# The low halves of streamed weight blocks: an accumulating DMA onto the negated high half in place of a subtraction on VectorE

## Chip, cores and metric

The kernel runs on one core of a Trainium2 chip. The metric is device time in microseconds (us) for one launch; lower is better. Engines are called by their names or by the letters of the profile: PE is TensorE's matmul queue, PEld its weight loads, DVE VectorE, ACT ScalarE, POOL GpSimd, SP SyncE.

## What is computed

A backbone of two layers (DEPTH = 2, D_MODEL = 1024, D_FF = 2816) for two groups of tokens that share all weights: a prompt of 128 tokens and a grid of 512 tokens. The kernel takes all 640 tokens through a layer together. In float32, cut to what matters:

```
h = rms_norm(x, norm1_g) * (1 + scale1) + shift1
z = h @ w_in            # conv streams, q, k, v, scan input, three gates
merged = (sigmoid(g_conv) * (y_conv @ w_proj_conv)
          + sigmoid(g_attn) * (y_attn @ w_proj_attn)
          + sigmoid(g_ssm) * (y_ssm @ w_proj_ssm))
x = x + gate1 * (merged @ w_out)
h = rms_norm(x, norm2_g) * (1 + scale2) + shift2
x = x + gate2 * ((silu(h @ w_ffn_gate) * (h @ w_ffn_up)) @ w_ffn_down)
```

The shifts, scales and gates are products of a condition vector with `w_ada` (1024 x 6144 in each layer).

## The kernel before

**Products of halves.** TensorE multiplies in the format float32r, which keeps fewer bits than float32. So every operand x is split as x = hi + lo, both of which float32r can hold, and a product is made of three: hi x hi, hi x lo, lo x hi. `gemm` (lines 732 to 740) does this for a tile of 128 output channels: for each of 8 input blocks k it issues hi of the weights with hi of the activations (two matmuls of 320 tokens), hi with lo (two) and lo with hi (two), so a tile has 48 matmuls, and the low half of the weights is first used by the fifth.

**The weight stream.** All weights come from HBM in 370 blocks of up to 128 x 1024 words (512 KB), in the order of use, which `order` lists (lines 284 to 360). `w_load` (line 365) takes one of three raw tiles (`wr`) and issues the load on SyncE's queue. `converter` (line 376) makes the two halves of a block in one of three tiles `wh` of 2 x 1024 words: a cast on ScalarE writes the high half, a subtraction on VectorE the low half. Then it calls `w_load` again: the next load must wait until its raw tile has been read. 308 blocks are converted in this way. 62 blocks of `w_ada` ("ada" blocks) are not: TensorE reads them raw, in eight matmuls with the condition vector (`ada_prod`), and the raw tile is free after that. They stand between the other blocks: one after each tile of the attention projection ("pa", `w_proj_attn`) and of the output projection ("o", `w_out`) in both layers, in layer 0 also between gate ("fg") and up ("fu") tiles of the feed-forward and in the convolution streams.

**What sets the order.** The program is written out by a planner. Main products are a generator (`layer`), side work (conversion, scan, attention) are further ones, and `pump` emits a piece of side work where the class `Clock` estimates that it can start. The estimates only set the order in which instructions stand in each engine's queue; each queue runs in that order. The converter may run up to two blocks ahead of the tile in use. In `Clock`, a DMA on GpSimd's queue counts as 1 us of that queue and 2 us more until its data is there. Every instruction is issued by a helper, so all of them have line 130 in the profile, and groups are told apart by the names of the tiles: `wr` raw block, `wh` halves, `bps` a tile in PSUM, `c` any tile of activations.

The conversion as it stands before:

```
            act.copy(hl[:, 0, :n], t[:, :n])
            yield hl, "dve"
            sub(hl[:, 1, :n], t[:, :n], f32(hl[:, 0, :n]))
            wtile[i] = [hl[:, r, :n].rearrange("p (k m) -> p k m", k=nr) for r in range(2)]
            w_load()
```

Of the kernel before, what the change touches and what calls it, by code (L numbers as in the profile page):

```python
# [11 lines left out]
OP = mybir.AluOpType  # L12
# [11 lines left out]
T = 8  # L24
# [33 lines left out]
class Clock:  # L58
    """estimated times (ns) of the instructions emitted so far; they only decide the order in which
    independent pieces of work are emitted"""  # L60
# [8 lines left out]
    def ring(self, tag, name, n):  # L69
        """a new PSUM tile takes the slot that is free first"""  # L70
        slots = self.rings.setdefault(tag, [None] * n)
        i = min(range(n), key=lambda j: self.free(slots[j]))
        self.avail[name] = self.free(slots[i])
        slots[i] = name
# [6 lines left out]
    def slot(self, tag):  # L81
        """when a tile can be had; side work ("b") leaves some PSUM tiles to the main products ("m")"""
        slots = sorted(self.free(x) for x in self.rings.get("b" if tag == "m" else tag, [None]))
        return slots[min(self.spare, len(slots) - 1) if tag == "b" else 0]

    def ready(self, needs):
        """when an instruction can start: needs are what it reads, its engine, and the tag of a PSUM tile it takes"""
# [23 lines left out]
class Engine:  # L111
    """forwards instructions to an engine and notes them in the clock"""
# [55 lines left out]
def trunk_kernel(ctx: ExitStack, tc: tile.TileContext, a):  # L168
# [86 lines left out]
    def split(x):  # L255
        """x = hi + lo exactly, both representable as float32r"""
# [5 lines left out]
    def split4(x):  # L262
        """x / 4 in the same way, from and to a tile of tokens"""
# [38 lines left out]
    def ada_gap(n):  # L302
        """blocks of the modulation products for times at which TensorE would wait"""
# [3 lines left out]
    def ada_n(key):  # L307
        """blocks of the modulation products after a tile"""
# [67 lines left out]
    def converter():  # L376
        for i, (key, src, nr, ncol) in enumerate(order):
# [10 lines left out]
            yield hl, "dve"  # L388
            sub(hl[:, 1, :n], t[:, :n], f32(hl[:, 0, :n]))
# [15 lines left out]
    class Side:  # L405
        """work beside the main products: a generator that yields, before each piece, what the first instruction
        of the piece needs (see Clock.ready), or a condition to wait for"""
# [23 lines left out]
    def pump(need=(), until=None):  # L431
        """emits the side work that can start before the main products"""
# [52 lines left out]
    # conditions between zeros: a window puts them on the rows of a slot  # L485
# [21 lines left out]
    def ada_flush(l=None, *vs):  # L507
        """the collected half vectors: rows to channels, bias, derived scales"""
# [30 lines left out]
    def ada_mm(k, w, c, start, stop):  # L539
        """a product of the conditions, on the rows of the slot in the column group of k"""  # L540
# [4 lines left out]
    def ada_step():  # L545
        """one block of the modulation products, of the weight stream"""
# [20 lines left out]
    def ada_pre(n):  # L567
        """loads blocks for the gaps"""
# [10 lines left out]
    def ada_fill(n):  # L579
        """blocks while TensorE would wait"""  # L580
# [6 lines left out]
    def ada_load():  # L587
        """next block of shift and scale of the first norm"""
# [11 lines left out]
    def ada_start():  # L600
        """shift and scale of the first norm, with plain float32 products"""
# [26 lines left out]
    def rstd(s, fill=(0,)):  # L628
        """reciprocal root mean square of each token, tokens on partitions"""
# [14 lines left out]
    def norm_rows(s, fill=(0, 0, 0), after=None):  # L644
        """reciprocal root mean squares on all partitions"""
# [14 lines left out]
    def norm(s, xs, sc, sh, fill=(0, 0, 0)):  # L660
        """h = x * rstd * sc + sh with the (sc, sh) of each group, split"""
# [36 lines left out]
    def place_x(xt, xs, sqs):  # L698
        """the residual stream, channels on partitions, and its squares"""
# [32 lines left out]
    def gemm(ps, w, c0, acts, first=True, last=True):  # L732
        """channel-major: ps[:, h, :HN] += w[:, :, c0:c0+128]^T @ acts, three products of the halves"""
# [17 lines left out]
    def gated(ps, x, gt, k):  # L751
        """x += gate * ps"""
# [14 lines left out]
    def pair_gemm(key1, key2, acts, evac1, evac2):  # L767
        """two tiles side by side, for activations that are still being made"""
# [20 lines left out]
    def blend(merged, m, th, ps):  # L789
        """merged[m] += (1 + th) * ps"""  # L790
# [6 lines left out]
    def branch(l, gk, pk, hs, ys, merged, spill=False):  # L797
        """merged += gate * projection; the first sum waits in DRAM for the second"""
# [63 lines left out]
    def hv(t):  # L862
        """[head of the pair, token tile, component]"""
        return t.rearrange("p (h i d) -> p h i d", h=2, i=NT)

    def token_major(key, hs, out):
        """raw projections of all tokens to 4 heads: two tiles of a head pair each"""
# [21 lines left out]
    def qk_norm(raw, which):  # L889
        """RMS over each head, gain, rotation of the sample tokens, in place"""  # L890
# [49 lines left out]
    def attn_prep(l, A, raws, preps, done):  # L940
        """per kv head, on partitions (hi, lo component): queries, keys; and values, (hi, lo) along the free axis"""
# [101 lines left out]
    def attn_scores(preps, scores, exps, done):  # L1043
        """exponentials, in the order in which they are used: per kv head those of the sample tokens, by head and
        query tile, then those of the prompt tokens"""
        for b in range(4):
# [18 lines left out]
            # prompt tokens, all four heads  # L1065
# [14 lines left out]
    def attn_turn(probs, turned, done):  # L1080
        """transposed probabilities: of pairs of query tiles, and of the prompt tokens of four heads"""
# [19 lines left out]
    def attn_split(turned, pts, done):  # L1101
        """both halves of the transposed probabilities"""
# [13 lines left out]
    def attn_out(preps, pts, done, ya):  # L1116
        """weighted sums of the values"""
# [44 lines left out]
    S = {}  # L1162

    def exp_acc(o, x, t, r, ki):
        """accurate exp of small tiles"""
# [35 lines left out]
    def ssm_layer(l):  # L1201
        """per-layer S5 parameters on partitions (direction, state)"""
# [42 lines left out]
        # coefficient (a - 1) / lambda  # L1245
# [27 lines left out]
        # unit phase and modulus of a^T  # L1273
# [28 lines left out]
        # powers a^0..a^8  # L1302
# [613 lines left out]
```

## Time and profile before

| | us |
|---|---|
| two timed runs | 2647.67 and 2642.18 |
| median | 2644.93 |
| span of the profiled execution, first to last instruction | 2643.2 |
| TensorE matmul busy | 2554.0 |
| VectorE busy | 1580.0 |
| ScalarE busy | 1016.2 |

The profile is of one execution. Its span is the time that rows are summed against; the two timed runs lie 1.0 us below and 4.5 us above it. A row of a group gives the engine, the operation, output<-input tiles, sizes and count, then the busy time, the mean duration of one, and the idle time of the engine just before these instructions with what ended it. A row of a timeline gives start and duration in us, and how many instructions of one kind follow each other. Matmuls overlap in their pipeline, so the mean duration of one is longer than the step from one to the next.

### The profile page before, as it was taken

The page shows a single profiled execution, that of the slowest core. Times are in us where ns is not written, and L with a number is a line of the kernel's source. Part 1 is how long each engine was busy: PE and PEld are TensorE (multiplying, and loading weights), DVE is VectorE, ACT ScalarE, POOL GpSimd, SP SyncE. Part 2 cuts the span into 40 slices and gives each one's busy share as a digit, 9 for nine tenths or more (in the row PEclk, how much of TensorE's full clock was granted, in tenths as well). Part 3 has the DMA queues.
Part 4 walks back from the last instruction along what each step waited for, and adds up shares of the span by engine and source line. Part 5 has one row for each costly group of instructions (what it writes and reads, how often), then busy time and mean ns, then how long its engine had stood idle before and what let it go on. Part 6 is the DMA issues. An engine that isn't in the chain of part 4 may idle for free. (4 is left out here: it accounts for less than half of the span.)

```text
span 2643.2 us, 44920 instructions
## 1 busy us (share of the span) xinstructions
PE 2554.0 (97%) x18683; PEld 2460.0 (93%) x18683; DVE 1580.0 (60%) x2982; ACT 1016.2 (38%) x1835; POOL 0.2 (0%) x4
## 2 busy tenths in 40 slices
PE   6999999999899999999989999999998999999998
PEld 4899999999888999999989999989998989999998
DVE  5888887788744433233677897578776453333333
ACT  4334336566622421122253333466664242212222
POOL 0000000000000000000000000000000000000000
PEclk8999999999999999999989999999999999999999
DMA  9433321121057233333334233212211633223222
GB/s 266 133 110 110 110 76 54 60 69 41 9 168 215 75 110 88 88 112 105 89 119 113 66 112 102 74 51 69 59 41 56 206 113 88 62 75 88 72 63 73
DMA packets 404411, 250.53 MB, mean 95 GB/s; under 512 B 57768, under 2 KB 392432, under 8 KB 404208
## 3 DMA queue, kind: packets, MB, share of 16 engines
q1 hardware_dynamic: 404208, 247.66, 31.9%
q8 instruction: 147, 2.41, 0.4%
q14 instruction: 56, 0.46, 0.1%
HBM read 227.49 MB, written 20.12 MB: 94 GB/s over the span
## 5 line engine op out<-in xcount | busy, mean ns | idle before, releaser
L130 PE MATMUL bps<-c,wh 128*128 128x320 f32 x12672 | 1952.1, 312 | 37.9 <-ACT c L130 18.4
L130 PEld LDWEIGHTS bps<-c,wh 128*128 128x128 f32 x12672 | 1876.4, 189 | 75.9 <-issue 25.1
L130 DVE TENSOR_TENSOR wh<-wr,wh 128x1024 fp32r<-128x1024 f32 (+2 forms) x308 | 353.8, 1153 | 223.6 <-ACT wh L130 213.8
L130 DVE TENSOR_TENSOR c<-c,c 128x512 f32<-128x512 f32 (+10 forms) x722 | 407.5, 590 | 71.6 <-ACT c L130 62.1
L130 ACT CAST wh<-wr 128x1024 fp32r<-128x1024 f32 (+2 forms) x308 | 303.7, 990 | 318.1 <-PE bps L130 177.9
L130 DVE SCALAR_TENSOR_TENSOR c<-c,bps 128x640 f32<-128x640 f32 (+1 forms) x108 | 83.2, 771 | 245.9 <-ACT c L130 169.6
L130 ACT CAST c<-c 128x640 fp32r<-128x640 f32 (+3 forms) x172 | 102.3, 621 | 327.0 <-DVE c L130 322.4
L130 DVE TENSOR_TENSOR c<-c,bps 128x640 f32<-128x640 f32 (+1 forms) x108 | 82.8, 769 | 205.9 <-PE bps L130 202.6
L130 PE MATMUL bps<-wh,c 128*128 128x256 f32 x1440 | 181.0, 284 | 2.0 <-ACT c L130 1.8
L130 ACT ACTIVATE c<-bps 128x640 f32<-128x640 f32 (+1 forms) x108 | 71.7, 664 | 285.3 <-PE bps L130 274.7
L130 PE MATMUL bps<-ident,c 128*128 128x128 f32 (+1 forms) x1115 | 159.1, 280 | 19.6 <-DVE c L130 7.4
L130 PEld LDWEIGHTS bps<-wh,c 128*128 128x128 f32 x1440 | 175.4, 191 | 2.7 <-ACT c L130 2.2
L130 PE MATMUL bps<-c,c 128*128 128x320 f32 (+2 forms) x960 | 159.5, 297 | 8.3 <-ACT c L130 4.5
L130 PEld LDWEIGHTS bps<-ident,c 128*128 128x128 f32 (+1 forms) x1115 | 132.6, 145 | 30.2 <-issue 8.9
L130 PEld LDWEIGHTS bps<-c,c 128*128 128x128 f32 x960 | 134.3, 191 | 13.4 <-ACT c L130 9.6
L130 ACT COPY c<-bps 64x256 f32<-64x256 f32 (+7 forms) x210 | 85.5, 445 | 155.8 <-PE bps L130 154.3
L130 ACT ACTIVATE c<-c 128x640 f32<-128x640 f32 (+4 forms) x93 | 65.3, 716 | 206.7 <-DVE c L130 206.5
L130 ACT ACTIVATE c<-bps,mx 128x640 f32<-128x640 f32 (+1 forms) x160 | 113.3, 713 | 36.1 <-DVE mx L130 35.6
L130 DVE TENSOR_REDUCE mx<-bps 128x1 f32<-128x640 f32 (+1 forms) x136 | 109.6, 809 | 26.4 <-PE bps L130 26.1
L130 DVE TENSOR_TENSOR pt<-bps,pt 128x640 fp32r<-128x640 f32 (+1 forms) x136 | 109.1, 810 | 15.3 <-ACT pt L130 14.5
L130 ACT CAST pt<-bps 128x640 fp32r<-128x640 f32 (+1 forms) x136 | 92.3, 687 | 26.6 <-PE bps L130 25.7
L130 PE MATMUL bps<-pt,c 128*128 128x256 f32 (+1 forms) x656 | 96.0, 292 | 2.9 <-DVE pt L130 2.1
(98 smaller groups left out, 1072.7 us busy)
## 6 DMA issues: line engine op xcount, KB each, us to landing
wr<-in_w_in_dram SPq DMA_DIRECT2D x104, 512.0 KB
wr<-in_w_ada_dram SPq DMA_DIRECT2D x62, 512.0 KB
wr<-in_w_ffn_gate_dram SPq DMA_DIRECT2D x44, 512.0 KB
wr<-in_w_ffn_up_dram SPq DMA_DIRECT2D x44, 512.0 KB
c<-in_w_ada_dram SPq DMA_DIRECT2D x68, 256.0 KB
wr<-in_w_ffn_down_dram SPq DMA_DIRECT2D x32, 384.0 KB
wr<-in_w_ffn_down_dram SPq DMA_DIRECT2D x32, 320.0 KB
wr<-in_w_proj_attn_dram SPq DMA_DIRECT2D x16, 512.0 KB
```

The lines of the kernel that those rows point to most:

```text
L130: res = f(*args, **kw)
```

## The change

The subtraction on VectorE goes. ScalarE now writes two tiles for each block: the cast as before, and the same block with the factor -1 into the place of the low half, which leaves the negated high half there. A DMA on GpSimd's queue then adds the raw block to it in place, so that block minus high half is left. The converter no longer stops between the two steps, so both copies stand together in ScalarE's queue. The raw tile is now read by ScalarE twice and by the DMA, and `w_load` waits for the DMA. The rest of the diff takes out docstrings and comments, which change no instruction.

```
@@ converter @@
             act.copy(hl[:, 0, :n], t[:, :n])
-            yield hl, "dve"
-            sub(hl[:, 1, :n], t[:, :n], f32(hl[:, 0, :n]))
+            act.activation(hl[:, 1, :n], t[:, :n], AF.Copy, scale=-1.0)
+            pool.dma_start(f32(hl[:, 1, :n]), t[:, :n], accum_op=OP.add)
             wtile[i] = [hl[:, r, :n].rearrange("p (k m) -> p k m", k=nr) for r in range(2)]
             w_load()
```

SyncE's queue in the attention projection of layer 0, before. A load waits for whatever read the raw tile last: DVE is the subtraction, PE the eight matmuls of an ada block; a DMAHW name is an earlier load by SyncE.

```order
L130 DMA wr<-in_w_ada_dram 128x4x256 [waits DMAHW6_49,PE_49]
L130 DMA wr<-in_w_proj_attn_dram 128x8x128 [waits DMAHW7_49,PE_49]
L130 DMA wr<-in_w_ada_dram 128x4x256 [waits DMAHW0_49,DVE_49]
L130 DMA wr<-in_w_proj_attn_dram 128x8x128 [waits DMAHW2_49,DVE_49]
L130 DMA wr<-in_w_ada_dram 128x4x256 [waits DMAHW1_49,PE_49]
L130 DMA wr<-in_w_proj_attn_dram 128x8x128 [waits DMAHW4_49,DVE_49]
L130 DMA wr<-in_w_ada_dram 128x4x256 [waits DMAHW3_49,PE_49]
L130 DMA wr<-in_w_proj_attn_dram 128x8x128 [waits DMAHW6_49,DVE_49]
```

The same place now; a DMASW name is an accumulating DMA of GpSimd's queue, Activation is ScalarE.

```order
L130 DMA wr<-in_w_ada_dram 128x4x256 [waits DMAHW6_49,PE_49]
L130 DMA wr<-in_w_proj_attn_dram 128x8x128 [waits DMAHW7_49,PE_49]
L130 DMA wr<-in_w_ada_dram 128x4x256 [waits DMAHW0_49,DMASW7_49,Activation_49]
L130 DMA wr<-in_w_proj_attn_dram 128x8x128 [waits DMAHW1_49,PE_49]
L130 DMA wr<-in_w_ada_dram 128x4x256 [waits DMAHW2_49,DMASW0_49,Activation_49]
L130 DMA wr<-in_w_proj_attn_dram 128x8x128 [waits DMAHW3_49,PE_49]
L130 DMA wr<-in_w_ada_dram 128x4x256 [waits DMAHW4_49,DMASW1_49,Activation_49]
L130 DMA wr<-in_w_proj_attn_dram 128x8x128 [waits DMAHW5_49,PE_49]
```

The two kinds of load have changed places: a projection block now goes into the tile that an ada block's matmuls free, an ada block into the tile that a conversion frees.

ScalarE's queue among the gate and up tiles of layer 0, before. `c<-bps` is the tanh of a gate tile, `c<-c` the cast of a hidden tile.

```order
L130 CAST wh<-wr 128x1024 [waits DMAHW7_49,Activation_49]
L130 ACTIVATE c_9729<-bps 128x640 [waits PE_49]
L130 CAST wh<-wr 128x1024 [waits DMAHW0_49,Activation_49]
L130 CAST c_9847<-c_9729 128x640 [waits DVE_49]
L130 CAST wh<-wr 128x1024 [waits DMAHW2_49,Activation_49]
```

And now:

```order
L130 CAST wh<-wr 128x1024 [waits DMAHW7_49,DMASW0_49,Activation_49]
L130 ACTIVATE wh<-wr 128x1024
L130 ACTIVATE c_9812<-bps 128x640 [waits PE_49]
L130 CAST wh<-wr 128x1024 [waits DMAHW0_49,DMASW1_49,Activation_49]
L130 ACTIVATE wh<-wr 128x1024
L130 CAST c_9932<-c_9812 128x640 [waits DVE_49]
L130 CAST wh<-wr 128x1024 [waits DMAHW2_49,DMASW2_49,Activation_49]
L130 ACTIVATE wh<-wr 128x1024
```

The order of casts and tile work is the same; the negated copy stands right behind each cast, and the cast of an up block still follows the cast of a hidden tile.

## Rows read from the trace of the kernel before

**Rows 1.** The page, part 1: busy us, share of the span, instructions.

```profile
PE 2554.0 (97%) x18683; PEld 2460.0 (93%) x18683; DVE 1580.0 (60%) x2982; ACT 1016.2 (38%) x1835; POOL 0.2 (0%) x4
```

**Rows 2.** Groups by form: shapes and count | busy us, mean ns | idle before.

```profile
L130 PE MATMUL bps<-c,wh 128*128 128x320 f32 x12672 | 1952.1, 312 | 37.9 <-ACT c L130 18.4 <-DVE c L130 9.5 <-DVE wh L130 7.2
...
L130 DVE TENSOR_TENSOR wh<-wr,wh 128x1024 fp32r<-128x1024 f32 x244 | 297.5, 1222 | 141.0 <-ACT wh L130 131.3
L130 ACT CAST wh<-wr 128x1024 fp32r<-128x1024 f32 x244 | 254.5, 1046 | 196.0 <-DMA wr<-in_w_proj_attn_dram 78.8 <-PE bps L130 77.0 <-DMA wr<-in_w_out_dram 32.5
...
L130 ACT CAST c<-c 128x640 fp32r<-128x640 f32 x116 | 81.8, 727 | 327.0 <-DVE c L130 322.4 <-issue 3.6
...
L130 ACT ACTIVATE c<-c 128x640 f32<-128x640 f32 x56 | 41.3, 742 | 169.3 <-DVE c L130 169.2
```

**Rows 3.** Waits: engine, waited for: us in total, times, longest us.

```profile
PE bps L130 <- ACT c L130: 30.1, 27, 5.9
...
PE bps L130 <- DVE c L130: 25.2, 29, 3.2
```

**Rows 4.** Waits of SyncE's DMA queue, the longest.

```profile
SPq L130 <- DVE wh L130: 1353.7, 254, 27.8
```

**Rows 5.** Timeline of PE, attention projection of layer 0.

```profile
744.45 0.64 PE L130 MATMUL bps<-wr,csT 128*32 128x256 f32 x8
745.02 7.30 PE L130 MATMUL bps<-c,wh 128*128 128x320 f32 x48
752.25 0.64 PE L130 MATMUL bps<-wr,csT 128*32 128x256 f32 x8
```

**Rows 6.** Timeline of SyncE's queue there: the issue of loads.

```profile
741.62 0.37 SPq L130 DMA_DIRECT2D wr<-in_w_proj_attn_dram  x1
745.15 0.37 SPq L130 DMA_DIRECT2D wr<-in_w_ada_dram  x1
747.58 0.37 SPq L130 DMA_DIRECT2D wr<-in_w_proj_attn_dram  x1
```

**Rows 7.** Timeline of ACT there: in brackets idle time before, and what ended it.

```profile
745.24 1.05 ACT L130 CAST wh<-wr 128x1024 fp32r<-128x1024 f32 x1 [4.91 <-DMA wr<-in_w_proj_attn_dram]
752.58 1.05 ACT L130 CAST wh<-wr 128x1024 fp32r<-128x1024 f32 x1 [6.29 <-DMA wr<-in_w_proj_attn_dram]
```

**Rows 8.** The chain that ended last, scan of layer 1: start us, us, what.

```profile
1465.78 1.78 DMA yd<-c
...
1468.01 2.88 DMA c<-yd
```

**Rows 9.** Stretches: us, busy us (count) by engine, granted clock, DMA share, GB/s.

```profile
1000.00:1100.00 100.00, 100.00 (x690) 98.79 (x689) 29.93 (x46) 19.05 (x24) 0.00 (x0) 1.00 0.31 89
784.00:840.00 56.00, 54.54 (x392) 50.38 (x392) 26.19 (x41) 12.19 (x14) 0.00 (x0) 1.00 0.81 254
713.00:719.00 6.00, 3.80 (x17) 3.07 (x16) 3.59 (x8) 4.14 (x8) 0.00 (x0) 0.78 0.00 0
```

**Rows 10.** Timeline of ACT, gate and up tiles of layer 0.

```profile
905.44 0.73 ACT L130 CAST c<-c 128x640 fp32r<-128x640 f32 x1 [7.02 <-DVE c L130]
906.07 1.05 ACT L130 CAST wh<-wr 128x1024 fp32r<-128x1024 f32 x1
```

**Rows 11.** Timeline of PE there.

```profile
911.51 0.64 PE L130 MATMUL bps<-wr,csT 128*32 128x256 f32 x8
912.08 14.34 PE L130 MATMUL bps<-c,wh 128*128 128x320 f32 x96
```

**Rows 12.** Timeline of DVE, attention projection of layer 0.

```profile
746.32 1.23 DVE L130 TENSOR_TENSOR wh<-wr,wh 128x1024 fp32r<-128x1024 f32 x1
```

## Prediction

> **What bounds the kernel now.** I read the page's busy times first, then the groups by form, the waits, SyncE's own waits, and last the timelines of the two places where a weight block is late.
>
> The busy times say that TensorE is the bound: 2554.0 of 2643.2 us, so all its idle time together is 89.2 us, while VectorE has 1580.0 us, ScalarE 1016.2 us and GpSimd nothing [rows 1]. That is the first thing to see: VectorE is not the bound, and whatever is taken off it can give back at most what TensorE waits for today. The groups give the price list: the subtraction takes 1222 ns for a block of 1024 words, the cast 1046 ns; the 12672 matmuls on weight halves have only 37.9 us of idle time ahead of them, 7.2 us of it until the subtraction [rows 2]. In the waits TensorE waited 30.1 us for ScalarE's tiles and 25.2 us for VectorE's [rows 3]. These 62.5 us are all that a faster VectorE could touch.
>
> SyncE's row is the second thing to see: its load queue stood 1353.7 us, 254 times, until a subtraction had freed a raw block [rows 4]. That costs nothing while the block comes back in time. How near it is to being late shows in the attention projection of layer 0. A tile's 48 matmuls and the 8 of an "ada" block make a period of 752.25 - 744.45 = 7.80 us [rows 5]. The load of a projection block is issued at 741.62 and at 747.58 us [rows 6], and the casts that wait for those loads start at 745.24 and 752.58 us [rows 7]: 3.62 and 5.00 us of landing, 4.3 in the mean. So each such block has load, cast and subtraction, about 4.3 + 2.3 us, in a chain of 6.6 us that must fit into 7.8 us. This is where a longer conversion goes onto the path.
>
> **What the change removes, adds and moves.** For each of the 308 converted blocks it removes the subtraction: 244 of 1024 words at 1.222 us [rows 2] and 64 of 640 or 768 words, which in proportion are 54 us: some 352 us in all from VectorE. Nearly all of it lies beside TensorE's work. What goes for certain is the 7.2 us of waits for a subtraction. Of the 55.3 us of waits for VectorE's and ScalarE's tiles I give back 10 us: VectorE comes sooner, but ScalarE, which releases the larger part, gets more to do.
>
> It adds to ScalarE a negated copy. The nearest rows are a cast of 640 words, 727 ns, and an activation of 640 words, 742 ns [rows 2]; so I take 1.02 x 1046 = 1.07 us for 1024 words, about 308 us in all. ScalarE has room for that in the mean (1016 + 308 of 2643 us), and in the dense stages it waits for TensorE; the price is that the low half starts 1.07 us later.
>
> It adds a DMA from GpSimd's queue, which reads the raw block and the negated half and writes the sum. GpSimd issues nothing today [rows 1], so nothing else is queued behind it there; but everything that waits for the low half or for the raw block now waits for this DMA to land. Its time from the end of the copy to landing, call it X, is the unknown of this case. Bound below: the shortest DMA on the chain of waits, 1.78 us from issue to landing for 160 KB [rows 8]. Bound above: two loads of 512 KB one after the other at the slower landing, 2 x 5.0 = 10.0 us. For the value I take one landing plus one more pass over the data, since two sources are read. A pass of 512 KB costs 524 KB / (89 GB/s / 0.31) = 1.83 us of all engines in the quiet stage [rows 9]; the landing is the 3.62 us of the load that had no other load just ahead. X = 5.5 us. The conversion, cast to landing, then takes C = 1.05 + 1.07 + 5.5 = 7.6 us instead of 2.3.
>
> The Trainium skill, "DMA: Bandwidth & Descriptors", section "Anatomy of one DMA — SWDGE (gpsimd) path", gives some 2.0 us plus bytes over 436 GB/s for a DMA issued by GpSimd; with the bytes counted twice that is an estimate of 4.4 us for this one. By it the stalls below would be about 70 us and the time about 2735 us; no run here shows such a DMA yet.
>
> What moves: the three raw slots are filled in another order. In the attention projection the projection block's load used to wait for the subtraction of the one before and the ada block's for TensorE; now it is the other way round, as the orders in the section on the change show. Step through it with T the start of a tile. The load is released by the ada product that ends at T, lands at T + 4.3, and its low half is there at T + 4.3 + 7.6 = T + 11.9. TensorE wants it at T + 7.8 + 0.6, because the first four matmuls of a tile use the high half. That is a stall of 3.5 us; the next block's load is issued during that stall and is only just late. So 3.5 us per two tiles, eight tiles in a layer: 14 us. In the output projection half of the loads wait for the conversion of the block before (C + L in one chain), which stalls four tiles by about 3.8 us each, 15 us; the first pair behind it, where the cast must wait for a slot, loses 7 us. 36 us per layer, 72 us for two.
>
> The gate and up tiles of layer 0 have an ada block between them. The up block's cast starts at 906.07 us, behind the cast of the hidden tile on ScalarE [rows 10], and its tile starts at 912.08 [rows 11], so the low half is wanted at 912.68: room for C = 6.6 us. At 7.6 that is 1.0 us for each of some 18 pairs, and 4 us at the last: 22 us. Layer 1 has no ada blocks there, and the cast lies two whole tiles ahead: nothing. In the same way, block by block from the casts and tile starts of the trace, the first tiles of both layers lose 15 us and the second down projection of layer 0, where the next layer's scan begins, 13 us. The scan and attention stages themselves have over 10 us of room per block and lose nothing here.
>
> Three more terms. A gap of TensorE lowers its clock: around a pause of 2.2 us out of 6 the granted clock was 0.78 [rows 9]; some 22 stalls are over 3 us and could cost 1.7 us each (a half-clock stretch of 3.4 us), of which I take 20 us in all, since part of it falls into the next wait. The engines of the DMA are busy 0.81 in the output projection [rows 9], and 3.7 us more per tile lengthens both landings there: 15 us. And SyncE's queue holds the scan's small transfers too, 1.78 and 2.88 us on the chain [rows 8], which now stand behind load waits that are 5 us longer: 8 us for the few that have no room.
>
> Sum: 72 + 22 + 15 + 13 = 122 us of stalls, - 7 - 10 + 20 + 15 + 8: + 148 us. The span is 2643.2 us, the two timed runs 2642.18 and 2647.67 (median 2644.93): 2645 + 148 = 2793 us. The stalls depend steeply on X: stepped in the same way they are 47 us at X = 3.6, 73 at 4.5, 122 at 5.5, 197 at 6.5, 320 at 8 and 502 at 10, because each stage joins when C passes its room.
>
> **The rivals.** *The transfer is hidden anyway (not slower).* Place: attention and output projections; price: stalls of 47 us or less, minus 17 us given back, plus 13 us for the small terms, so about 2688 us; at X = 2.5 it would be equal to today. It decides for X up to some 3.6 us. For it: the slack rows are real (5.27 us between the end of the subtraction, 746.32 + 1.23, and the tile, 752.25 + 0.57) [rows 5, 12], and the small DMAs land in 1.8 to 2.9 us [rows 8]. Against it: a plain load of the same size, which reads one source, takes 3.6 to 5.0 us.
>
> *The accumulating DMA is slow.* If two passes do not overlap, or the issue by software takes a microsecond or two more, X is 8 us or over and every pair of gate and up tiles stalls: 320 to 502 us of stalls, less the 17 us given back and with some 60 us for the small terms, which grow with the stalls: 3010 to 3190 us. For it: nothing in this trace shows an accumulation, and VectorE and the DMA engines are both busy in the stages that count. The Trainium skill, "SBUF — State Buffer", section "Who interferes with whom", says that a DMA issued by GpSimd waits for its descriptors while VectorE holds the shared port in its two-port modes; that would add to X, and no run here shows it. Against it: in the quiet stage the DMA engines are busy only 0.31 [rows 9], so two passes have room beside the loads.
>
> *VectorE was the bound after all (faster).* All of TensorE's 62.5 us of waits for the subtraction, VectorE and ScalarE would have to go and no stall come: 2583 us. Against it stand the second copy on ScalarE and every length of X that the rows allow.
>
> **How the numbers follow.** Forecast (X from 3.9 to 7.5): 0.60. Slow DMA: 0.19. Hidden: 0.18. VectorE the bound: 0.03. Over 2% is 53 us, about what a measurement of this kernel can tell from no change. In the forecast's own cases those under X = 4.0 stay inside it, hence slower 0.78, same 0.19, faster 0.03. The range goes from the hidden case, 2688, to X = 8, which is 2645 + 320 - 17 + 60 = 3008 us: 2685 to 3010 us.
>
> **What would show it.** Right: TensorE's idle time grows from 89 us to over 200 us, nearly all of it until a DMA that writes the weight halves, in the two projections and in the gate and up tiles of layer 0; VectorE's busy time falls to about 1228 us and ScalarE's rises to about 1325 us; the gate and up tiles of layer 1 run as closely as before. Wrong: a landing under 4 us from the end of the copy, or over 8; stalls spread over layer 1's feed-forward too; or idle time that still ends on VectorE.

## The result, and the profile after

The changed kernel takes 2826.65 us (median of two runs, 2822.53 and 2830.76), the kernel before 2644.93 us (2642.18 and 2647.67): a ratio of 1.0688, 95% interval 1.0643 to 1.0734. Slower by 182 us, where 148 were forecast. The profiled execution took 2830.76 us, its span is 2829.0 us: 185.8 us more than the span before.

The page's busy times, as [rows 1]:

```profile
PE 2619.6 (93%) x18683; PEld 2513.6 (89%) x18683; DVE 1256.5 (44%) x2690; ACT 1281.4 (45%) x2127; POOL 265.7 (9%) x312
```

TensorE's idle time is span less busy time: 2829.0 - 2619.6 = 209.4 us, 120.2 more than before. Its busy time rose too, by 65.6 us for the same 18683 matmuls. These two numbers make up the whole difference, and they call for two explanations. VectorE lost 323.5 us of work, ScalarE took on 265.2 us, and neither is near being the bound.

The groups by form, as [rows 2]:

```profile
L130 PE MATMUL bps<-c,wh 128*128 128x320 f32 x12672 | 2008.2, 317 | 142.1 <-DMA wh<-wr 115.3 <-ACT c L130 15.6 <-DVE c L130 10.9
...
L130 POOL DMA_DIRECT2D wh<-wr x308 | 265.5, 862 | 2534.6 <-ACT wh L130 2209.6 <-PE bps L130 157.6 <-ACT c L130 53.5
L130 ACT ACTIVATE wh<-wr 128x1024 fp32r<-128x1024 f32 x244 | 258.1, 1058 | 0.0
```

The idle time ahead of the matmuls on weight halves went from 37.9 to 142.1 us, and 115.3 us of it now end on the accumulating DMA. The negated copy takes 1058 ns and never finds ScalarE idle ahead of it, since it stands right behind its cast.

The waits of TensorE and of SyncE's queue, as [rows 3, 4]:

```profile
PE bps L130 <- DMA wh<-wr: 115.3, 53, 6.6
PE bps L130 <- DVE c L130: 33.1, 31, 4.8
PE bps L130 <- ACT c L130: 29.9, 27, 4.7
...
SPq L130 <- DMA wh<-wr: 1886.0, 284, 29.6
```

The wait for the subtraction is gone, but the waits for VectorE's and ScalarE's tiles did not shrink, though VectorE has a fifth less to do. SyncE's loads now wait 1886.0 us for the accumulating DMA, where they waited 1353.7 us for the subtraction.

The DMA itself, first its queue on the page beside that of the loads and stores (packets, MB, share of 16 engines):

```profile
q1 hardware_dynamic: 404208, 247.66, 29.9%
q0 software_dynamic: 44352, 151.01, 29.0%
```

Then, from the view of tile wh, the time from issue to landing over all 308:

```profile
DMA to landing us min/median/max: 3.6/4.8/9.6
```

The 151 MB of the accumulation occupy the DMA engines for as long as 247.66 MB of loads and stores do. What the landing does to the path shows in the output projection of layer 0, in the timeline of all engines but DVE and PEld (start us, us):

```profile
845.29 8.14 PE L130 MATMUL bps<-c,wh 128*128 128x320 f32 x44 [2.36 <-DMA wh<-wr]
...
848.55 1.05 ACT L130 CAST wh<-wr 128x1024 fp32r<-128x1024 f32 x1 [5.04 <-DMA wr<-in_w_out_dram]
849.51 1.05 ACT L130 ACTIVATE wh<-wr 128x1024 fp32r<-128x1024 f32 x1
850.85 0.86 POOL L130 DMA_DIRECT2D wh<-wr  x1 [13.79 <-ACT wh L130]
...
855.52 6.71 PE L130 MATMUL bps<-c,wh 128*128 128x320 f32 x44 [0.75 <-DMA wh<-wr]
855.54 0.37 SPq L130 DMA_DIRECT2D wr<-in_w_ada_dram  x1
```

From the end of the negated copy (849.51 + 1.05 = 850.56) to the landing, which lets TensorE go on at 855.52, it is 4.96 us: 0.29 to the issue and 4.67 to the landing. The same landing frees the raw tile, and 0.02 us later SyncE issues the load that waited for it. Loads, conversions, landings and TensorE's tiles form a chain here, each waiting for another.

Stretches of before and after: attention and output projection of layer 0, and the second half of gate and up tiles of layer 1 (us, busy us by engine, granted clock, DMA share, GB/s). Before:

```profile
717.10:783.50 66.40, 64.37 (x452) 59.25 (x454) 27.37 (x32) 17.00 (x22) 0.00 (x0) 0.97 0.43 127
783.50:860.00 76.50, 73.45 (x562) 64.59 (x561) 36.59 (x69) 18.13 (x23) 0.00 (x0) 0.98 0.71 220
...
2394.70:2549.60 154.90, 154.90 (x1059) 154.90 (x1058) 52.69 (x56) 35.34 (x43) 0.00 (x0) 1.00 0.25 73
```

And after:

```profile
744.20:827.10 82.90, 69.47 (x449) 63.83 (x449) 18.05 (x24) 21.17 (x25) 6.60 (x8) 0.90 0.57 140
827.10:932.40 105.30, 83.92 (x562) 74.17 (x561) 26.29 (x60) 30.56 (x38) 8.02 (x10) 0.87 0.82 215
...
2579.30:2734.10 154.80, 154.80 (x1057) 154.80 (x1057) 26.64 (x34) 55.90 (x65) 18.94 (x22) 1.00 0.66 150
```

The projections grew by 16.5 and 28.8 us, and TensorE's granted clock there fell from 0.97 and 0.98 to 0.90 and 0.87. The second half of layer 1's gate and up tiles, where the conversion runs two tiles ahead, did not lose a microsecond, though the DMA share rose from 0.25 to 0.66 there. So where the conversion has that room, an accumulation costs TensorE nothing.

### The profile page after: what moved, and what is told of

Read it like the earlier page. It is cut to its first block, busy times and chain, and to the rows that moved or that the text cites. A ratio compares the mean times of both kernels' runs of the same rounds, so it can differ in the third digit from the quotient of the medians.

```text
span 2829.0 us, 45945 instructions
## 1 busy us (share of the span) xinstructions
PE 2619.6 (93%) x18683; PEld 2513.6 (89%) x18683; DVE 1256.5 (44%) x2690; ACT 1281.4 (45%) x2127; POOL 265.7 (9%) x312
## 3 DMA queue, kind: packets, MB, share of 16 engines
q1 hardware_dynamic: 404208, 247.66, 29.9%
## 5 line engine op out<-in xcount | busy, mean ns | idle before, releaser
L130 PE MATMUL bps<-c,wh 128*128 128x320 f32 x12672 | 2008.2, 317 | 142.1 <-DMA wh<-wr 115.3
L130 PEld LDWEIGHTS bps<-c,wh 128*128 128x128 f32 x12672 | 1921.6, 193 | 193.1 <-DMA wh<-wr 132.1
L130 POOL DMA_DIRECT2D wh<-wr x308 | 265.5, 862 | 2534.6 <-ACT wh L130 2209.6
L130 ACT ACTIVATE wh<-wr 128x1024 fp32r<-128x1024 f32 (+2 forms) x308 | 308.4, 1001 | 0.0
L130 PE MATMUL bps<-c,c 128*128 128x320 f32 (+2 forms) x960 | 166.1, 306 | 19.6 <-DVE c L130 11.0
L130 DVE SCALAR_TENSOR_TENSOR c<-bps,g2T,c 128x128 f32<-128x128 f32 (+2 forms) x96 | 36.3, 433 | 205.3 <-PE bps L130 205.3
```

The source lines that it names most:

```text
L130: res = f(*args, **kw)
```

## The experiments

Two mechanisms could make the 186 us. *Latency*: TensorE waits for the low half itself. *Loads*: the raw tile is held until the DMA has landed, and the DMA's traffic runs beside the loads, so the next block comes late whatever TensorE does. Beside them stood ScalarE's second copy and TensorE's clock. Stage by stage, the runs against the kernel before (us, from the first matmul of a stage's first block to that of the next stage; "first" is u, conv and gate tiles, "scan" attention, scan and their gates, "ffn" gate, up and down tiles; the last column is 2 x (1 - mean granted clock) x span, the time at the lower of the clock's two levels, 1.2 of 2.4 GHz; before it is 69 us, with a mean of 0.987):

| run | us | first 0 | scan 0 | pa 0 | o 0 | ffn 0 | first 1 | scan 1 | pa 1 | o 1 | ffn 1 | at low clock |
|---|---|---|---|---|---|---|---|---|---|---|---|---|
| after | 2826.65 | 30.8 | -2.2 | 16.5 | 28.8 | 38.5 | 22.2 | 3.3 | 16.2 | 26.6 | 5.6 | 215 |
| e1 late use | 2741.48 | 31.4 | -19.7 | 7.7 | 22.8 | 20.5 | 10.1 | -2.5 | 4.4 | 16.5 | 4.1 | 131 |
| e2 late use, before | 2664.86 | 15.1 | -9.7 | -1.9 | 1.0 | 5.9 | 7.7 | -5.1 | -2.0 | 1.0 | 4.1 | 74 |
| e4 hold + traffic | 2727.48 | 4.8 | -2.0 | 5.1 | 30.0 | 12.5 | 4.0 | 6.1 | 6.0 | 21.9 | 0.8 | 131 |
| e5 traffic | 2666.93 | 5.7 | -1.8 | 0.0 | 3.6 | 5.4 | 2.4 | 6.2 | 0.0 | 1.9 | 0.8 | 85 |
| e9 hold | 2664.91 | 0.6 | -2.4 | 0.6 | 11.7 | 1.0 | -1.4 | 5.7 | 0.0 | 5.8 | 0.0 | 85 |
| e7 e1, four raw tiles | 2688.19 | 26.3 | -17.5 | -2.5 | 10.4 | 13.5 | 8.2 | -1.6 | -2.5 | 6.5 | 4.1 | 107 |
| e8 pa and o subtract | 2735.63 | 28.2 | -0.1 | 0.0 | 0.0 | 35.0 | 19.7 | 3.5 | 0.0 | 0.0 | 5.1 | 131 |
| e10 second copy alone | 2709.48 | 8.4 | 17.3 | 1.2 | 1.3 | 7.4 | 3.9 | 16.0 | 0.0 | 2.8 | 5.6 | 114 |
| e11 only with room | 2658.22 | 1.1 | -6.1 | -0.2 | -0.1 | -0.3 | -0.1 | 12.7 | 0.7 | 0.0 | 5.3 | 74 |

A stage's sum also holds side work that the planner moved there, so the first and scan columns are read together.

**e1 and e2: the low half used later.**

```
-            for n, (r, s) in enumerate(((0, 0), (0, 1), (1, 0))):
+            for s in range(2):
                 for h in range(2):
-                    mm(ps[:, h, 0:HN], w[r][:, k, c0:c0 + 128], x[s][:, h * HN:(h + 1) * HN],
+                    mm(ps[:, h, 0:HN], w[0][:, k, c0:c0 + 128], x[s][:, h * HN:(h + 1) * HN],
...
+        for k in range(K):
...
+            for h in range(2):
+                mm(ps[:, h, 0:HN], w[1][:, k, c0:c0 + 128], x[0][:, h * HN:(h + 1) * HN],
```

> Of the changed kernel, only the order of the matmuls within a tile is changed: the 32 that use the high half of the weights come first, the 16 that use the low half last, so that the low half is wanted 32 matmuls (about 4.9 us) after the tile's start, not 4 (0.6 us). The same products are summed, in another order. Theory (the low half is late by about 7.5 us counted from its cast, and the clock falls in the gaps this makes): room grows by 4.3 us, PE's idle time before the bps<-c,wh matmuls on DMA wh falls from 115 us to under 15, half-clock time falls from 218 us back to 70 to 100 us, time 2640 to 2680 us. Rival (the transfers take DMA engines and SBUF from the loads, or raw tiles are held longer): idle on DMA wh moves to loads of wr, time above 2760. Rival (the second copy on ScalarE delays tile work): time above 2720, idle of PE on ACT c well over 30 us.

> The same order of matmuls in the kernel before, with its subtraction on VectorE: the control for the run above. Theory: its low half is not late, so nothing to gain but the 7 us that PE waited for the subtraction: 2625 to 2650 us. If the order of matmuls is worth something by itself, it shows here and is taken off the run above.

Measured: 2741.48 us (1.0374, 1.0358 to 1.0389), 85 us less than the changed kernel; the control 2664.86 us (1.0088, 1.0071 to 1.0104), 23 us *more* than the kernel before in the same comparison: the new order has a cost of its own. Both expectations were missed, the theory's for e1 by 61 us and the control's by 15. The wait of e1 for the DMA, which was expected under 15 us:

```profile
PE bps L130 <- DMA wh<-wr: 32.0, 22, 3.3
```

Latency is real: 83 us of waits for the DMA are gone with the order of the matmuls (and the side work that the planner placed by it). But e1 stays 77 us above its control, where the upper ends of the two expectations were 30 apart: of the 182 us, some 105 went with the late use and 77 did not. Half of what is left sits in the output projections (22.8 and 16.5 us), which points to the loads.

**e3: the negated copy first.**

```
-            act.copy(hl[:, 0, :n], t[:, :n])
             act.activation(hl[:, 1, :n], t[:, :n], AF.Copy, scale=-1.0)
             pool.dma_start(f32(hl[:, 1, :n]), t[:, :n], accum_op=OP.add)
+            act.copy(hl[:, 0, :n], t[:, :n])
```

> Of the changed kernel, ScalarE makes the negated copy first and the high half second, so the accumulating DMA starts 1.05 us earlier and the high half is there 1.05 us later. Theory: the late low half lands 1.05 us earlier at each of the about 45 stalled tiles, stalls fall from 115 to about 70 us and the clock loss with them by 30: 2740 to 2765 us. Rivals (contention of the transfers, or the time of the second copy): no change, 2815 to 2835 us.

Measured: 2781.89 us (1.0527, 1.0495 to 1.0559). 45 us less for a start that is 1.05 us earlier, 43 us for each us, but 17 us short of the expected range. TensorE's waits for the DMA fell from 115.3 to 77.8 us, near the 70 expected. What the high half, which is now the later one to be made, costs in return is not shown. The prediction's steepness was 49 us between X of 4.5 and 5.5.

**e4, e5, e6, e9: hold and traffic apart**, all on the kernel before with its subtraction, and with two activation tiles less to make room. `spare` and `mark` are tiles that nothing reads.

```
             sub(hl[:, 1, :n], t[:, :n], f32(hl[:, 0, :n]))
+e4:         pool.dma_start(spare[:, :n], t[:, :n], accum_op=OP.add)
+e5:         pool.tensor_copy(mark, f32(hl[:, 1, 0:1]))
+            pool.dma_start(spare[:, :n], spare[:, :n], accum_op=OP.add)
+e6:         pool.dma_start(mark[:, i % 4], t[:, 0:32], accum_op=OP.add)
+e9:         the line of e6 twice
```

> The kernel before, with its subtraction on VectorE, and beside it an accumulating DMA of each raw block onto one spare tile that nothing reads (two activation tiles fewer, to make room for it). The raw tile is held until that DMA has read it, as in the changed kernel; TensorE waits for nothing new. Theory: the traffic and the held raw tiles cost at most 25 us: 2640 to 2675. Rival (contention with the loads, or the load chain): 2740 us or more, with PE and ACT waiting for loads of wr.

Measured: 2727.48 us (1.0321, 1.0289 to 1.0353). The expectation of at most 25 us was wrong by 60, and its rival's 2740 us was not reached. SyncE's waits in the output projection of layer 0 (106.6 us long), then the same in the kernel before (76.5 us long):

```profile
SPq L130 <- DMA spare<-wr: 74.9, 11, 9.8
```

```profile
SPq L130 <- PE bps L130: 23.6, 8, 5.1
SPq L130 <- DVE wh L130: 18.7, 8, 3.8
```

The loads stand for 74.9 us behind raw tiles that the DMA still reads, where they stood for 42.3 us; TensorE waits for no accumulation and yet loses 30 us there. Two flaws of e4: each DMA also waits for the one before, because they write one tile; and it reads the raw block alone, so it starts when the load has landed and not behind the conversion. A block of the output projection:

```profile
814.27 1.04 ACT L130 CAST wh<-wr 128x1024 fp32r<-128x1024 f32 x1 [8.54 <-DMA wr<-in_w_out_dram]
814.70 0.86 POOL L130 DMA_DIRECT2D spare<-wr  x1 [12.46 <-DMA wr<-in_w_out_dram]
```

Worked out from the traces, the last reader is done with a raw tile of the attention and output projections 5.0 and 6.3 us after the cast's start in e4 (median of 16 blocks each), 7.4 and 7.6 us in the changed kernel, 2.3 us in the kernel before. So e4 holds the tile for less long than the change does.

> As e4 (the kernel before, with its subtraction, and an accumulating DMA of 512 KB beside each conversion), but the DMA adds the spare tile to itself (zeros), so it holds no raw tile: its traffic alone, on the same queue at the same place, with one small GpSimd copy ahead of it. Theory H (what e4 lost, 85 us, came from the raw tile that is held until the DMA has landed, which delays the next load): 2640 to 2670 us, the output projection of layer 0 back near its 76.5 us. Theory C (contention: the transfers slow the loads by themselves): 2700 to 2735, that stage still 95 us or more.

> As e4, but the DMA that reads each raw tile moves only 32 words of each partition (16 KB) to a small tile: the raw tile is held until it has landed, with hardly any traffic. Its landing should take 2 to 3 us in place of 5. Theory H: 40 to 60 per cent of the 85 us, 2670 to 2695 us. Theory C: 2640 to 2655 us.

> As e6 (the kernel before, each raw tile held until a small DMA of 16 KB has read it), but with two such DMAs one behind the other onto the same words, so that the raw tile is held for two landings, 4 to 5 us, about as long as by a DMA of 512 KB (5 us), and still with hardly any traffic. If e4's 85 us came from the length of the hold alone, this one is at 2700 us or more. If it takes both (a DMA of 512 KB lands late beside the loads, and the load behind it starts late and runs beside the next), 2650 to 2680 us, with the output projection of layer 0 under 90 us (e4: 106).

Measured: e5 2666.93 us (1.0104, 1.0084 to 1.0125); e6 2650.66 us (1.0040, 1.0024 to 1.0056); e9 2664.91 us (1.0089, 1.0070 to 1.0107). The landings of e6 and e5, issue to landing:

```profile
DMA to landing us min/median/max: 2.0/2.1/6.5
```

```profile
DMA to landing us min/median/max: 3.6/5.7/9.6
```

e5 fell in the range of theory H, e6 in that of C, e9 in that of both. But e6 hardly tests a hold: its DMA, too, starts with the load's landing, and in most blocks it has landed before the cast begins. In the projections its raw tiles are free 2.6 and 4.7 us after the cast's start, those of e9 after 5.3 and 8.3 us.

Traffic alone costs 27 us, the hold of e9 23, and e4, which has both, 85: more than the 50 of the parts, although e9 holds the tiles longer there than e4. So neither the traffic nor the length of the hold makes e4's loss by itself. That the two feed each other (a DMA lands late beside loads, the next load starts late behind it and runs beside the next DMA) fits. Its first link shows in e6: 16 KB land after 2.1 us in the median, but in the output projection of layer 0, where the DMA engines are 0.77 busy, after this:

```profile
DMA to landing us min/median/max: 2.3/4.3/4.9
```

A rival to that account is the order of the loads, which the edits moved as well: in the output projection of layer 0 SyncE's queue never waits for TensorE in e4, five times in e9, six times in the changed kernel. No run holds this order fixed, so its share of the 85 us is open.

**e7: four raw tiles** in e1, for one activation tile and some second buffers less.

```
-WR = 3
+WR = 4
```

> As e1 (the changed kernel, low products last in a tile) with four raw tiles in place of three (one activation tile less, and the second buffer of a few small vectors taken away, to make room). Theory H: the load of the next block no longer waits for the accumulating DMA, the 77 us that e1 stands above e2 shrink to 30 or less: 2665 to 2700 us. Theory C: the engines of the DMA are as busy as before, 2725 to 2745 us.

Measured: 2688.19 us (1.0184, 1.0167 to 1.0201), 53 us less than e1 at the same traffic; TensorE's waits for the accumulating DMA are down to this:

```profile
PE bps L130 <- DMA wh<-wr: 7.7, 6, 2.3
```

The wait for a raw tile was two thirds of the 77 us. A fourth tile in e2 was not run; but TensorE waits only 7.6 us for weight halves there, so without the DMA it has little to give. 23 us remain against e2, in the first tiles, the output projections and the second down projection of layer 0.

**e8: subtraction kept in pa and o.**

```
+            if key[0] not in ("pa", "o"):
                 act.activation(hl[:, 1, :n], t[:, :n], AF.Copy, scale=-1.0)
                 pool.dma_start(f32(hl[:, 1, :n]), t[:, :n], accum_op=OP.add)
+            else:
+                yield hl, "dve"
+                sub(hl[:, 1, :n], t[:, :n], f32(hl[:, 0, :n]))
```

> The changed kernel with VectorE's subtraction kept in the 32 blocks of the attention and output projections (pa, o), and the accumulating DMA in the other 276. Theory (the loss sits where an ada block shortens the room and the loads are dense; pa and o lost 16.5 + 28.8 + 16.2 + 26.6 = 88 us of 185): those four stages come back to within 4 us each of before, 2735 to 2760 us. Rival (a loss spread over all blocks, from ScalarE's second copy or from the traffic): 2790 us or more.

Measured: 2735.63 us (1.0365, 1.0344 to 1.0385). The same two stretches of layer 0, of the same 66.40 and 76.50 us as in the kernel before:

```profile
743.30:809.70 66.40, 64.37 (x452) 59.25 (x455) 27.37 (x32) 17.00 (x22) 0.00 (x0) 0.97 0.43 127
809.70:886.20 76.50, 73.45 (x562) 64.43 (x561) 34.25 (x67) 20.19 (x25) 1.72 (x2) 0.98 0.79 234
```

32 of 308 blocks made half of the loss, and what is outside them kept its own. e8 tells the place alone: in these blocks the late landing, the traffic and the order of the loads all go at once.

**e10: the second copy alone.**

```
             act.copy(hl[:, 0, :n], t[:, :n])
+            act.activation(hl[:, 1, :n], t[:, :n], AF.Copy, scale=-1.0)
             yield hl, "dve"
             sub(hl[:, 1, :n], t[:, :n], f32(hl[:, 0, :n]))
```

> The kernel before, with ScalarE's negated copy written into the low half ahead of VectorE's subtraction, which then writes over it: ScalarE's second copy alone, no DMA. The conversion is 1.07 us longer and ScalarE has 308 us more to do. Theory (the copy costs only through the low half being later, and 3.4 us would still be hidden): 2640 to 2655 us, ScalarE busy 1280 to 1325 us. Rival (ScalarE's tile work is held up): over 2670 us, PE waiting for ACT c by 20 us more than in the kernel before.

Measured: 2709.48 us (1.0257, 1.0239 to 1.0276): the theory said 2640 to 2655. The longest of VectorE's waits on weight halves, then TensorE's waits:

```profile
DVE wh L130 <- ACT wh L130: 349.5, 197, 6.9
...
PE bps L130 <- ACT c L130: 39.4, 42, 6.9
...
PE bps L130 <- DVE wh L130: 23.9, 15, 3.9
```

In the kernel before, VectorE had 213.8 us in 90 such waits. Here every subtraction stands in VectorE's queue behind a copy that ends 1.05 us later, and all other work of VectorE stands behind the subtraction. The time is that of the rival, its sign is not: TensorE waits 39.4 us for ScalarE's tiles, 9 us more than before, where the rival wanted 20. Half of the loss lies in the scan stages (17.3 and 16.0 us), where the changed kernel lost next to nothing. So this run is no measure of the copy in the changed kernel: it points to the longer hand-over between two queues, and leaves open what the copy by itself does there.

**e11: the accumulation only where there is room** (k, v, q, glu, gs, ps; gate, up and down tiles of layer 1), 128 blocks.

> The accumulating DMA only where a block's low half has many us of room: the attention's and the scan's tiles (k, v, q, glu, gs, ps) in both layers, and the gate, up and down tiles of layer 1; VectorE's subtraction in all other blocks. Theory: no low half is late, no load is late, VectorE has some 200 us less to do where it does not bound: 2635 to 2655 us, the same as the kernel before within 0.5 per cent. If every accumulation had a cost of its own (0.6 us a block by the 185 us over 308 blocks), over 2740 us.

Measured: 2658.22 us (1.0063, 1.0050 to 1.0075), 3 us over the expected range. No price of 0.6 us for each block (128 would cost 77 us, and 16 are lost), but no gain either: VectorE's busy time fell by 136.5 us to 1443.5 us, and TensorE took nothing of it. So no version found here beats the kernel before.

**e12: TensorE kept at work in the stalls.**

```
+                for _ in range(fill if k == 0 and n == 2 else 0):
+                    pe.eng.matmul(ps[:, 0, 0:HN], zw, x[0][:, 0:HN], start=False, stop=False, skip_group_check=True)
```

> The changed kernel, with 16 to 24 extra matmuls (weights of zeros, onto the tile's own sums, which they leave as they are) between the fourth and the fifth matmul of eight tiles of pa and o in each layer, where TensorE waits 2.4 to 5.9 us for the low half: 160 of them a layer, 24.3 us at full clock, so TensorE is kept at work in the stalls. Theory (the clock falls because of these gaps, and the time at half clock is lost on the path): half-clock time falls by 40 us or more from 218, and the time by 10 to 30 us, to 2797 to 2817. Rival 1 (the low half's arrival is paced by the chain of loads and conversions, not by TensorE's speed): half-clock time falls as much, but the time stays at 2820 to 2835. Rival 2 (the clock does not follow the gaps): half-clock time as before, time 2827 to 2850.

Measured: 2835.55 us (1.0723, 1.0708 to 1.0737), no less than the changed kernel; the time at the lower clock fell from 215 to 176 us. In the attention projection of layer 0, lines of TensorE, SyncE's queue and ScalarE in the changed kernel:

```profile
790.42 8.23 PE L130 MATMUL bps<-c,wh 128*128 128x320 f32 x44 [3.38 <-DMA wh<-wr]
798.59 0.64 PE L130 MATMUL bps<-wr,csT 128*32 128x256 f32 x8
799.28 0.37 SPq L130 DMA_DIRECT2D wr<-in_w_proj_attn_dram  x1
...
803.32 1.05 ACT L130 CAST wh<-wr 128x1024 fp32r<-128x1024 f32 x1 [9.15 <-DMA wr<-in_w_proj_attn_dram]
...
811.32 8.05 PE L130 MATMUL bps<-c,wh 128*128 128x320 f32 x44 [3.51 <-DMA wh<-wr]
```

And of TensorE in e12, where line 745 is the filling and the helper has moved to line 131:

```profile
789.40 3.68 PE L745 MATMUL bps<-c,zw 128*128 128x320 f32 x24
792.92 6.62 PE L131 MATMUL bps<-c,wh 128*128 128x320 f32 x44
...
801.17 6.71 PE L131 MATMUL bps<-c,wh 128*128 128x320 f32 x44 [0.28 <-DMA wh<-wr]
...
814.27 6.72 PE L131 MATMUL bps<-c,wh 128*128 128x320 f32 x44 [1.39 <-DMA wh<-wr]
...
825.99 8.26 PE L131 MATMUL bps<-c,wh 128*128 128x320 f32 x44 [3.64 <-DMA wh<-wr]
```

Behind a gap 44 matmuls take 8.05 to 8.23 us, behind the filling 6.62 to 6.72: the gap had lowered the clock. What TensorE gained, about 1.5 us a tile, did not come off the time. New waits stand in tiles that had none (0.28 and 3.64 us), and both attention projections are some 5 us longer than in the changed kernel.

That fits rival 1, but it does not show it for the changed kernel, because the edit also moved the loads. SyncE's waits in that projection, in the changed kernel (760.0 to 827.1) and in e12 (762.0 to 834.2):

```profile
SPq L130 <- PE bps L130: 43.3, 6, 8.7
SPq L130 <- DMA wh<-wr: 13.4, 3, 5.9
```

```profile
SPq L131 <- DMA wh<-wr: 64.1, 7, 12.1
SPq L131 <- PE bps L131: 5.5, 2, 4.3
```

In e12 the loads follow landings. In the changed kernel TensorE is in the chain: the load at 799.28 waits for the ada product behind the slow tile (798.59 + 0.64 = 799.23), and its block is the one that TensorE waits for until 811.32. A tile that takes 1.6 us longer at the lower clock puts that load off by as much. So in this place the lower clock lies on the path, and how much time it costs in all stays open. Also, in some tiles the filling is longer than the gap that it replaces, which hides a small gain.

## Why the prediction was right, and where it was off

**The mechanism** was the forecast one. TensorE was the bound and stayed it; what VectorE gave up was worth nothing (e11); the low half came late where an ada block shortens the room. Of the signs, TensorE's idle time came (209.4 us, over 200), and layer 1's gate and up tiles run as closely as before behind their second gate tile. VectorE's 1256.5 and ScalarE's 1281.4 us lie near the 1228 and 1325 forecast. Of the idle time only 115.3 us end on the DMA: nearly all of its growth, but not nearly all of it.

**X**, the time from the end of the negated copy to the landing, was taken as 5.5 us. Measured: 4.8 us from issue in the median and 0.3 us ahead of it, 5.1 us; 3.6 to 9.6 us over all blocks from issue. The choice between bounds of 1.78 and 10.0 was good. The Trainium skill, "DMA: Bandwidth & Descriptors", section "Anatomy of one DMA — SWDGE (gpsimd) path", has a fixed part of 2.0 us; e6 agrees, with a median of 2.1 us for 16 KB. The estimate of 4.4 us worked out from that page of the Trainium skill, with the bytes counted twice, is 0.5 us below the profile's 4.9 us for 512 KB, and its time of 2735 us is 92 us below the measured one. The same skill's "SBUF — State Buffer", section "Who interferes with whom", has GpSimd wait for VectorE's two-port modes; GpSimd's issue had a median of 862 ns and a maximum of 1002 ns over 308, so no such wait shows in the issue; in which modes VectorE ran, the trace does not show.

**The stalls, 122 us**: the waits for the DMA are 115.3 us. That this is so near is in part luck: between the forecast's own 73 us at X = 4.5 and 122 at 5.5, the measured 5.1 stands for some 100, and places that came out larger and smaller offset each other. By place (from a tile's start to its fifth matmul, less the 0.6 us between them, which gives a little more than the waits; in the first tiles the waits): 14.5 and 13.5 us in the attention projections (14 forecast), every second tile, as stepped; 20.9 and 20.4 us in the output projections (15), in seven tiles rather than four; the pair behind each of these (7) did not stall, but the next gate tile did, by 3.7 us in both layers; 25.4 us in the first tiles of both layers (15); 6.2 us in the second down projection of layer 0 (13). For the gate and up tiles of layer 0 the sum was near, the tile was wrong: 20.1 us ahead of gate tiles (those 3.7 us among them) and 2.7 us ahead of up tiles. Where it had nothing, in the scan's projections, TensorE waits 3.1 us. The timeline shows why the gate tiles of layer 0 are late:

```profile
969.87 1.05 ACT L130 CAST wh<-wr 128x1024 fp32r<-128x1024 f32 x1
...
975.88 8.16 PE L130 MATMUL bps<-c,wh 128*128 128x320 f32 x52
976.02 1.04 ACT L130 CAST wh<-wr 128x1024 fp32r<-128x1024 f32 x1
976.76 0.37 SPq L130 DMA_DIRECT2D wr<-in_w_ada_dram  x1
...
977.23 0.45 SPq L130 DMA_DIRECT2D wr<-in_w_ffn_up_dram  x1
978.31 0.86 POOL L130 DMA_DIRECT2D wh<-wr  x1 [5.29 <-ACT wh L130]
...
985.07 3.19 PE L130 MATMUL bps<-c,wh 128*128 128x320 f32 x20 [1.03 <-DMA wh<-wr]
```

The up block (cast at 969.87) is there in time: its 52 matmuls run through without a break. The gate block's cast at 976.02 stands right behind a tile that has just been freed; its DMA runs beside two loads issued 1.55 and 1.08 us ahead of it and takes 6.8 us from issue. The room was read from the rows, but X was taken as one number, and it depends on the loads beside it.

**What was given back, 17 us**: the 7 us of waits for the subtraction went. The 10 us for VectorE's and ScalarE's tiles did not come: 33.1 + 29.9 = 63.0 us against 55.3 [rows 3].

**The clock, 20 us**, is the term that was mis-sized. TensorE's busy time rose by 65.6 us. The forecast charged 22 long stalls with 1.7 us each and cut that by half, because a part falls into the next wait. The time at the lower level went from 2 x 0.013 x 2643.2 = 69 us to 2 x 0.038 x 2829.0 = 215 us, and half of the 146 us between is 73 us. The clock records of the trace have 15 stretches at that level before and 39 after: 24 more, near the 22 of the forecast, but 146 / 24 = 6.1 us long, which is 3 us of lost work each. 120.2 us of idle time and 65.6 us of clock are the span's 185.8 us; forecast were 128 (122 - 17 + 15 + 8) and 20. So the idle time was near and the clock came to over three times its term. Neither number says what the span would be at full clock. Where the next load waits for TensorE's ada product, as in the attention projection, a slow tile delays it, and the halving had no ground there; e12 cannot tell the rest, since its loads stand in another order.

In the pa and o stages 14 + 15 = 29 us of stalls were forecast in each layer. Of the 45.3 us lost there in layer 0, 29.7 are idle time and 15.6 TensorE's longer busy time (5.1 and 10.5 in the stretches above). So the stalls are there as forecast, e8 puts them there, and the rest is the clock's. The 15 us for busy DMA engines were not measured by themselves; e4 to e9 point to what they stand for, the chain of loads and landings.

**The rivals.** *Hidden* and *VectorE the bound* fell with X and with the busy times. *The accumulating DMA is slow* wanted X over 8 us: only the longest landings come to that, beside loads. The price set on SyncE's small transfers, 8 us, was not measured by itself.

**Open**: the 23 us between e7 and e2, which the second copy, the traffic, or both may make; what the lower clock costs in time; and how the 85 us of e4 divide between hold, traffic and the order of the loads.

## What to carry to other kernels

When work goes from an engine to a DMA, what counts is the time from the last input to landing and how long the source buffer is held, not the engine time saved: step both through the tightest stages, and take the landing from a moment at which that stage's loads run too. Measure hold and traffic together, since here 23 and 27 us apart were 85 us at once, and look at what each load waits for in every test: an edit beside a stream of loads can move their order too. Where a stage is paced by a chain of transfers, see whether TensorE releases one of them. If it does, a lower clock lies on the path; if not, it may be a symptom.

## What was not expected of the hardware

- An accumulating DMA of 512 KB from SBUF to SBUF lands 4.9 us after its issue in the median, one of 16 KB after 2.1 us. 151 MB of it took 29.0% of the DMA engines' span, 247.66 MB of loads and stores 29.9%: by the profile's count of bytes 1.6 times as much for each.
- TensorE's clock fell behind short waits too: after a gap of 3.38 us the next 44 matmuls took 8.23 us, with the gap filled 6.62 us.
- The landing of 16 KB took 2.1 us in the median, and 4.3 us in the output projection of layer 0, where the DMA engines were 0.77 busy.
